# An in projection with tokens stationary, in groups of four tiles, turned by VectorE and a scratch buffer

## The chip, the cores and the metric

The kernel runs on one core of one Trainium2 chip. The metric is device time in microseconds (us) of one execution, as the median of several runs. The engines are TensorE (PE; PEld is its weight load), VectorE (DVE), ScalarE (ACT), GpSimd (POOL) and SyncE (SP), which issues most transfers. SBUF is the working memory, PSUM holds matmul sums.

## The reference, cut to what matters

One decoder layer over 256 tokens with 2,048 features, all in float32: a mixer, a memory cross-attention and a SwiGLU FFN, each behind an RMS norm, with residual adds and a last norm. The change lies in the mixer:

```python
proj = h @ w_in                                  # h: (256, 2048), w_in: (2048, 11296)
z, xbc, dt_raw, sc_u, sc_b, sc_c = split(proj)   # 2048, 3072, 32, 2048, 2048, 2048
xbc = silu(causal_dwconv(xbc, ssd_conv_w) + ssd_conv_b)       # 4 taps along the tokens
xs, bm, cm = split(xbc)                          # 2048, 512, 512
y = ssd_chunked(xs, softplus(dt_raw + dt_bias), -exp(a_log), bm, cm) + xs * d_skip
y_ssd = grouped_rmsnorm(y * silu(z), ssd_norm, 4)
v = sc_b * causal_dwconv(sc_c * sc_u, sc_conv_w)              # 3 taps
y_sc = grouped_rmsnorm(v, sc_norm, 16)
h = h + concatenate([y_ssd, y_sc]) @ w_out       # w_out: (4096, 2048)
```

## The kernel before, in words

**Precision.** Every float32 factor is split into a high part, rounded to the fp32r format, and a low part, the rest. A product is made as high x high + low x high + high x low, in fp32r matmuls summed in PSUM.

**The weight stream.** All weights come in one stream of blocks of 128 x 1024 floats (512 KB), in the order of `stream_plan` (L69). `load_to` (L146) issues the loads on SP, up to `AHEAD` = 6 blocks ahead into 6 raw buffers. `split_to` (L157) makes each block's high part on ACT (L167) and its low part on DVE (L168), with 4 buffers for each.

**Units.** The work is a row of units (`unit`, L273) of two blocks each. A unit issues loads, splits and its matmuls; after its first part it calls `step` (L253), which moves every running process (a Python generator, one for each chain of later work) on to its next `yield`. A `yield` so means "one unit later", and it is counted by hand so that what a chain puts on PE finds its data ready. PE and SP run in program order as written (L114); the order on ACT, DVE and POOL is made by the framework's scheduler.

**The in projection** (L718 to L778) makes 88 tiles of 128 features x 256 tokens, features on partitions. The order is `mixer_order` (L47): for each of 4 head groups its B and C tile, then z and xs tiles, and between them short convolution tiles (c, u, b). The first four tiles, `FIRST`, run in halves of K. For a tile the weights are stationary. For each of 16 blocks of K, `mm_hi` (L293, matmul at L296) multiplies the weights' high part with the tokens' high and low parts at once (512 columns: 256 of each), and `mm_lo` (L298, L302) multiplies the weights' low part with the tokens' high part (256 columns). A tile takes one PSUM buffer of 512 columns, of which there are 4 (`acc`). `evac_sum` (L191) adds its two halves: a copy on ACT (L194) and an addition on DVE (L195).

**The chains behind a tile.** `conv_post` (L610; four taps, L614 to L618), `z_post` (L718), `scc_post`, `scu_post`, `scb_post` (L742 to L771), `b_post`, `c_post` and `xs_post` (L621 to L698). They put small single precision matmuls on PE, between the parts of later units: turns of xs tiles (L660), score products (L634), the scan (L676, L678), and for the norms turns (L202, in `flip`) and broadcasts (L244, in `bcast`). `norm_group` (L700) ends by writing features for the out projection into `ys`: 0 to 15 from the heads, 16 to 31 from the short convolutions. The last short convolutions have fewer yields, so that they end in time.

**The out projection** (L898) takes 4 column blocks n of 512; for each, 16 weight blocks c, block c reading `ys[2c]` and `ys[2c + 1]`. Here tokens are stationary and weights move (`tok_mm`, L791): for each half of a block and each of two token blocks three matmuls of 512 columns (L798 to L800), into two PSUM buffers. `wo_post` adds the residual (L814), and for blocks 0 to 2 turns the result onto features: `turn_blocks` (L818, transposes of 32 x 32 blocks on DVE, L822) into one of 2 buffers, `put` (L825) writes 512 KB to a scratch buffer in DRAM, and `get` (L831) reads it back in four transfers of 128 KB with features on partitions. The gate and up stage (L1074) uses the same `tok_mm` and, behind each up block, the same three steps.

Of the kernel before, what the change touches and what calls it, by code (L numbers as in the profile page):

```python
# [13 lines left out]
F32 = mybir.dt.float32  # L14
# [6 lines left out]
T = 256  # L21
# [21 lines left out]
UT, SBT, SCT = 0, 16, 32  # L43
FIRST = (BT, CT, ZT, ZT + 1)


def mixer_order():  # L47

    o, sc = [], iter(range(16))

    def short_conv():
        j = next(sc)
        return [("scc", "b", SCT + j, j), ("scu", "b", UT + j, j), ("scb", "b", SBT + j, j)]

    for g in range(4):
        if g:
            o += [("B", "a", BT + g, g), ("C", "a", CT + g, g)]
        for t in range(4 * g, 4 * g + 4):
            if ZT + t not in FIRST:
                o.append(("z", "a", ZT + t, t))  # L60
            o.append(("xs", "a", XT + t, t))
            if t % 4:
                o += short_conv()
    for _ in range(4):
        o += short_conv()
    return o


def stream_plan():  # L69

    p = []
    p += [(("k0",), 512), (("v0",), 512)]
    for kt in range(1, KT):
        p.append((("kv", kt), 1024))
    p += [(("a", t, c), 1024) for c in range(2) for t in FIRST]
    for _, m, t, _ in mixer_order():
        p += [((m, t, c), 1024) for c in range(2)]
    for n in range(4):
        p += [(("wo", n, c), 1024) for c in range(KT)]
    p += [(("q", t, c), 1024) for c in range(2) for t in range(4)]  # L80
    p += [(("o", n, c), 1024) for n, c in [(0, 0), (1, 0), (0, 1), (1, 1), (2, 0), (2, 1), (3, 0), (3, 1)]]
    for n in range(FN):
        for m in "gu":
            p += [((m, n, c), 1024) for c in range(KT // 2)]
    for n in range(4):
        p += [(("d", n, c), 1024) for c in range(FT // 2)]
    return p


def trunk(tc, wst, vecs, xp, xtp, mp, wdt_in, nfin, outp):  # L90
# [9 lines left out]
    with ExitStack() as ctx:  # L100
# [139 lines left out]
        def bcast(r):  # L240
# [5 lines left out]
            return ps  # L246


        now = [0]
# [48 lines left out]
        def mm_lo(ps, key, acts, k0, stop):  # L298
            _, l = fin(key)
            n = plan[index[key]][1] // 128  # L300
            for k in range(n):
                mm(ps[:, 0:T], l[:, k * 128:k * 128 + 128], acts[k0 + k][:, 0:T], start=False, stop=stop and k == n - 1)  # L302

        def pair_parts(a, b):

            def los_():
                mm_lo(*a[:4], a[5])
                mm_lo(*b[:4], b[5])

            return [([a[1], b[1]], lambda: mm_hi(*a[:5])), ([b[1]], lambda: mm_hi(*b[:5])), ([a[1], b[1]], los_)]  # L310

# [308 lines left out]

        def b_post(g, ps):  # L621
            bct[g] = slot()
            conv_post(ps, 16 + g, bct[g][:, 0:T], ("B", g))
            return
            yield

        def c_post(g, ps):
            conv_post(ps, 20 + g, bct[g][:, T:], ("C", g))
            yield
# [20 lines left out]

        def xs_post(g, j, ps):
            t = 4 * g + j
            xs = slot()
            conv_post(ps, t, xs[:, 0:T], ("xs", t))
            yield
# [44 lines left out]
        def norm_group(items, sums, sq, n, key):  # L700
            r = inv_rms(sums(sq), n)
            yield
            if key != ("sc", 15):
                yield
            rb = bcast(r)
# [22 lines left out]
        def std_unit(m, t, post):  # L728

            ps = acc()  # L730
            unit(pair_parts((ps, (m, t, 0), xn, 0, True, False), (ps, (m, t, 1), xn, 8, False, True)), post(ps))

        fps = [acc() for _ in FIRST]
        for c in range(2):
            for i in (0, 2):
                posts = [b_post(0, fps[0]), c_post(0, fps[1])] if i == 0 else [z_post(0, fps[2]), z_post(1, fps[3])]
                unit(pair_parts(*[(fps[k], ("a", FIRST[k], c), xn, 8 * c, c == 0, c == 1) for k in (i, i + 1)]),
                     posts if c else None)

        scc, scv = {}, {}  # L740

        def scc_post(j, ps):  # L742
            c = slot()
            evac_sum(ps, c[:, 0:T])
            scc[j] = c
            return
            yield

        def scu_post(j, ps):
            u = tmp()  # L750
            evac_sum(ps, u)
            c = scc[j]
            tt(u, u, c[:, 0:T], ALU.mult)
            a = c[:, T:]
            ts(a, u, v("sw", 3 * j + 2), None, ALU.mult)
# [6 lines left out]

        def scb_post(j, ps):
            u = tmp()
            evac_sum(ps, u)
            a = scv[j]
            tt(a, a, u, ALU.mult)
            yield
            if j < 14:
                yield  # L770
            yield from norm_group([(a, v("nsc", j), 16 + j)], feature_squares, a, 128, ("sc", j))  # L771

        posts = {"B": b_post, "C": c_post, "z": z_post, "scc": scc_post, "scu": scu_post, "scb": scb_post,
                 "xs": lambda t, ps: xs_post(t // 4, t % 4, ps)}
        for kind, m, t, j in mixer_order():
            if kind == "B":
                procs.append(decay(j))
            std_unit(m, t, lambda ps: posts[kind](j, ps))  # L778

# [10 lines left out]

        def tok_mm(ps, key, blocks, tbs, start, stop, ks=(0, 1)):  # L791

            h, l = fin(key)
            for i in ks:
                w = slice(i * 512, i * 512 + 512)
                for tb in tbs:
                    ah, al = blocks(i, tb)
                    mm(ps[tb], ah, h[:, w], start=start and i == ks[0], stop=False)  # L798
                    mm(ps[tb], ah, l[:, w], start=False, stop=False)  # L799
                    mm(ps[tb], al, h[:, w], start=False, stop=stop and i == ks[-1])  # L800

        def side_blocks(tiles, k0):

            def blocks(i, tb):
                a = tiles[k0 + i]
                return a[:, tb * 128:tb * 128 + 128], a[:, T + tb * 128:T + tb * 128 + 128]

            return blocks

        def add_to_res(n, accs, sums):  # L810

            for tb in range(2):
# [3 lines left out]
                act(j, h, AF.Square, accum_out=sums[:, tb, n:n + 1])  # L816

        def turn_blocks(src):  # L818

            t = bp.tile([128, 1024], F32, tag="b", name=nm("b"))  # L820
            for tb in range(2):
                nc.vector.transpose(t[:, tb * 512:tb * 512 + 512], src[tb])  # L822
            return t

        def put(t):  # L825

            w = drp.tile([2, 128, 512], F32, tag="w", name=nm("w"), bufs=2)
            nc.sync.dma_start(w.rearrange("t p k -> p t k"), t.rearrange("p (t k) -> p t k", t=2))
            return w

        def get(w):  # L831


            d = fp.tile([128, 1024], F32, tag="f", name=nm("f"))
            for b in range(4):
                nc.sync.dma_start(d[32 * b:32 * b + 32, :].rearrange("p (x c) -> p x c", x=8),
                                  w.rearrange("t (a i) k -> i (t a) k", a=4)[:, :, 128 * b:128 * b + 128])
            return d.rearrange("p (x f j) -> p f x j", x=8, f=4)

# [57 lines left out]

        for n in range(4):  # L898
            accs = [acc(), acc()]
            for c in range(0, KT, 2):  # L900
                unit([([("wo", n, k)],
                       lambda k=k: tok_mm(accs, ("wo", n, k), side_blocks(ys, 2 * k), (0, 1), k == 0, k == KT - 1))
                      for k in (c, c + 1)], wo_post(n, accs) if c == KT - 2 else None)

# [310 lines left out]
def _weights(i):  # L1215
# [8 lines left out]
    blk["a"] = tiles(w_in[:, 0:5120], 8)  # L1224
    blk["b"] = tiles(w_in[:, 5152:], 8)
    blk["q"] = tiles(_turned(np.asarray(i["w_q"])[0], 3), 8)
    rows = {m: (_turned(np.asarray(i[k])[0]) if m == "d" else np.asarray(i[k])[0]).reshape(-1, 2, 128, i[k].shape[-1] // 512, 512).transpose(3, 0, 2, 1, 4)
            for m, k in (("wo", "w_out"), ("o", "w_o"), ("g", "w_gate"), ("u", "w_up"), ("d", "w_down"))}
    wk, wv = np.asarray(i["w_k"])[0], np.asarray(i["w_v"])[0]
    plan = stream_plan()  # L1230
    out = np.empty(sum(128 * w for _, w in plan), np.float32)
    p = 0
    for key, w in plan:
        m = key[0]
        if m == "k0":
            c = wk[0:128]
# [58 lines left out]
```

## Time and profile before

| what | value |
|---|---|
| median of 3 runs | 1544.58 us (1544.18 to 1544.87) |
| the profiled execution: its own time | 1543.5 us |
| the profiled execution: its span | 1541.8 us |
| in projection, from the span's start | about 54.5 to 581.7 us |
| out projection | about 581.7 to 757 us |

The span is what the trace covers; the execution's own time has 1.7 us more around it. The page gives each engine's busy time, the granted clock of PE, the chain of work that ended last and groups of instructions; other views give the waits, the instructions in order of time and busy times by window. A duration of a PE matmul is modelled and overlaps the next one's, so PE's pace is read from the distance between starts. Lines such as L296 are lines of the kernel before.

### The profile page before, as it was taken

The numbers are of one execution on the slowest core, as the hardware profiler recorded it, in microseconds if no ns is written. First come the engines' busy times: TensorE is split into PE (matmuls) and PEld (weight loads), VectorE is DVE, ScalarE is ACT, GpSimd is POOL, SyncE is SP. The second block draws the span as 40 slices with busy tenths as digits, with TensorE's granted clock in tenths as the row PEclk, the third lists the DMA queues.
The fourth block names the chain that finished last, engine by engine and source line by source line (L and its number), as shares of the span: only waits on it lengthen the run. The fifth ranks groups of instructions, "written<-read, shape, count | busy, mean of one in ns | idle before, by whom it ended". The sixth has DMA issues, their size and how long they took to land.

```text
span 1541.8 us, 20228 instructions
## 1 busy us (share of the span) xinstructions
PE 1528.6 (99%) x7607; PEld 1282.6 (83%) x7607; DVE 930.3 (60%) x1239; ACT 807.0 (52%) x1158; POOL 44.9 (3%) x65
## 2 busy tenths in 40 slices
PE   9999999999999999999999999999999999999997
PEld 7888888888888888888888888888888888888886
DVE  5967786786776675555566555555455555455453
ACT  6685774775774454444465444444444444444343
POOL 0001300100100000000000000000000000000000
PEclk9999999999999999999999999999999999999999
DMA  9765655655655556777645666666766666656652
GB/s 349 251 201 186 218 176 180 217 178 177 209 186 168 181 173 208 237 235 231 193 134 180 218 219 224 214 206 202 232 221 221 218 227 198 239 192 195 196 193 96
DMA packets 112001, 315.33 MB, mean 205 GB/s; under 512 B 11008, under 2 KB 33952, under 8 KB 111904
## 3 DMA queue, kind: packets, MB, share of 16 engines
q1 hardware_dynamic: 102704, 306.66, 61.1%
q10 hardware_dynamic: 9200, 7.39, 1.6%
q8 instruction: 59, 0.97, 0.3%
q14 instruction: 38, 0.31, 0.1%
HBM read 304.53 MB, written 9.49 MB: 204 GB/s over the span
## 4 chain that ended last, share of the span: by engine, by line
PE 95%; DMA 1%; ACT 1%; issue 1%; SPq 0%; DVE 0%; POOLq 0%; POOL 0%; ACTq 0%
PE a L296 22%; PE a L800 20%; PE a L799 20%; PE a L798 20%; PE a L302 11%; DMA r<-in_w_dram 1%; PE m L676 1%; ACT h L167 0%; PE m L202 0%; PE m L244 0%; PE a L518 0%; PE m L868 0%; PE m L678 0%; PE m L660 0%; PE m L926 0%
## 5 line engine op out<-in xcount | busy, mean ns | idle before, releaser
L168 DVE TENSOR_TENSOR l<-r,h 128x1024 fp32r<-128x1024 f32 (+2 forms) x555 | 656.0, 1191 | 509.1 <-ACT h L167 419.9
L167 ACT CAST h<-r 128x1024 fp32r<-128x1024 f32 (+2 forms) x555 | 564.7, 1022 | 617.2 <-PE a L800 463.3
L798 PE MATMUL a<-h,s 128*128 128x512 f32 x1343 | 524.1, 390 | 0.0
L800 PE MATMUL a<-h,s 128*128 128x512 f32 x1343 | 522.7, 389 | 0.0
L799 PE MATMUL a<-l,s 128*128 128x512 f32 x1343 | 522.6, 389 | 0.0
L296 PE MATMUL a<-s,h 128*128 128x512 f32 x1472 | 370.4, 397 | 0.3 <-ACT h L167 0.3
L296 PEld LDWEIGHTS a<-s,h 128*128 128x128 f32 x1472 | 265.5, 188 | 52.9 <-issue 2.6
L800 PEld LDWEIGHTS a<-h,s 128*128 128x128 f32 x1343 | 252.1, 188 | 52.3
L799 PEld LDWEIGHTS a<-l,s 128*128 128x128 f32 x1343 | 252.1, 188 | 52.1
L798 PEld LDWEIGHTS a<-h,s 128*128 128x128 f32 x1343 | 252.1, 188 | 52.0
L302 PEld LDWEIGHTS a<-s,l 128*128 128x128 f32 x1472 | 188.9, 191 | 7.8
L302 PE MATMUL a<-s,l 128*128 128x256 f32 x1472 | 191.4, 282 | 0.0
L194 ACT COPY t<-a 128x256 f32<-128x256 f32 x96 | 35.1, 369 | 37.0 <-PE a L302 36.7
L617 DVE SCALAR_TENSOR_TENSOR t<-t,vec,t 128x255 f32<-128x255 f32 (+2 forms) x72 | 34.7, 482 | 6.1 <-ACT t L614 5.3
L237 POOL TENSOR_TENSOR rr<-rv,half 128x2 f32<-128x2 f32 x24 | 16.6, 692 | 643.5 <-DVE rv L236 626.6
L195 DVE TENSOR_TENSOR t<-a,t 128x256 f32<-128x256 f32 x76 | 31.8, 418 | 5.2 <-ACT t L194 4.0
L518 PE MATMUL a<-s,h 128*128 128x512 f32 x64 | 23.9, 404 | 1.0 <-DVE s L182 0.5
L1123 POOL TENSOR_TENSOR fr<-fr,half 128x1 f32<-128x1 f32 x2 | 1.1, 550 | 716.8 <-DVE fr L1122 716.8
L1049 ACT ACTIVATE g<-a,fscale 128x512 f32<-128x512 f32 x22 | 15.0, 689 | 9.9 <-PE a L800 9.9
L519 PE MATMUL a<-s,l 128*128 128x256 f32 x64 | 18.4, 287 | 0.7 <-DVE l L168 0.7
L236 DVE TENSOR_SCALAR rv<-rv 128x2 f32<-128x2 f32 x24 | 4.0, 168 | 24.4 <-ACT t L229 24.1
L618 ACT ACT_TABLE_LOAD x12 | 15.4, 1283 | 6.2 <-DVE t L617 3.1
(172 smaller groups left out, 683.2 us busy)
## 6 DMA issues: line engine op xcount, KB each, us to landing
r<-in_w_dram SPq DMA_DIRECT2D x535, 512.0 KB, 4.1
w<-b SPq DMA_DIRECT2D x14, 512.0 KB, 3.3
f<-w SPq DMA_DIRECT2D x56, 128.0 KB, 4.4
s<-acsT ACTq DMA_DIRECT2D x24, 256.0 KB, 6.3
s<-in_xt_dram SPq DMA_DIRECT2D x16, 256.0 KB, 6.0
s<-in_x_dram SPq DMA_DIRECT2D x8, 256.0 KB, 7.2
s<-in_m_dram SPq DMA_DIRECT2D x7, 256.0 KB, 7.2
s<-in_nfin_dram SPq DMA_DIRECT2D x4, 256.0 KB, 7.5
```

What stands on the lines that cost most here:

```text
L167: nc.scalar.copy(h[:, c], r[:, c])
L168: tt(l[:, c], r[:, c], h[:, c].bitcast(F32), ALU.subtract)
L194: nc.scalar.copy(t, ps[:, T:])
L195: tt(dst, ps[:, 0:T], t, ALU.add)
L296: mm(ps, h[:, k * 128:k * 128 + 128], acts[k0 + k], start=start and k == 0, stop=False)
L302: mm(ps[:, 0:T], l[:, k * 128:k * 128 + 128], acts[k0 + k][:, 0:T], start=False, stop=stop and k == n - 1)
L518: mm(kacc[t], h[:, t * 128:t * 128 + 128], a, start=s, stop=False)
L519: mm(kacc[t][:, 0:T], l[:, t * 128:t * 128 + 128], a[:, 0:T], start=False, stop=e)
L617: stt(a[:, d:], u[:, 0:T - d], v("cw", 4 * ct + k), a[:, d:], ALU.mult, ALU.add)
L798: mm(ps[tb], ah, h[:, w], start=start and i == ks[0], stop=False)
L799: mm(ps[tb], ah, l[:, w], start=False, stop=False)
L800: mm(ps[tb], al, h[:, w], start=False, stop=stop and i == ks[-1])
```

## The change

- `mixer_groups` replaces `mixer_order`: the same 88 tiles in the same order, the four of `FIRST` at the head, cut into 22 groups of four.
- The weights of a group are laid out as 512 columns, permuted on the host so that DVE's 32 x 32 transposes and the strided read give whole features. A group has 8 blocks, each with two blocks of K.
- Each group runs through `tok_mm` into two PSUM buffers, in 4 units. Groups 0 and 1 alternate by halves of K.
- Behind a group, `group_post` turns the sums (one unit later), writes them (one later), reads them back (one later) and starts the four tiles' chains, one per unit, or all four at once for the last three groups.
- `evac_sum` goes from the in projection's chains. `conv_post` copies its tile from the read-back buffer on ACT; z, c, u and b read it in place. The shortened yields of the last short convolutions go.
- `turn_blocks` has 1 buffer in place of 2, `get` 3 in place of 2.
- The out projection reads blocks c = 0 to 13 of n = 0 and of n = 1, then c = 14 and 15 of both, then n = 2 and 3 as before.

```diff
-def mixer_order():
+def mixer_groups():
...
-    return o
+    return [o[i:i + 4] for i in range(0, len(o), 4)]
+
+def out_order():
+    return ([(n, c) for n in range(2) for c in range(14)] + [(n, c) for n in range(2) for c in (14, 15)]
+            + [(n, c) for n in (2, 3) for c in range(KT)])
...
-        bp = E(tc.tile_pool(name="blocks", bufs=2))
-        fp = E(tc.tile_pool(name="feat", bufs=2))
+        bp = E(tc.tile_pool(name="blocks", bufs=1))
+        fp = E(tc.tile_pool(name="feat", bufs=3))
...
-        def conv_post(ps, ct, dst, key):
+        def conv_post(src, ct, dst, key):
             u = tmp()
-            evac_sum(ps, u)
+            nc.scalar.copy(runs(u), src)
...
-        def z_post(t, ps):
-            u = tmp()
-            evac_sum(ps, u)
+        def z_post(t, src):
             sz = slot()[:, 0:T]
-            act(sz, u, AF.Silu)
+            act(runs(sz), src, AF.Silu)
...
-            tt(u, u, c[:, 0:T], ALU.mult)
+            tt(runs(u), src, scc.pop(j), ALU.mult)
...
+        def group_post(n, accs):
+            t = turn_blocks(accs)
+            yield
+            w = put(t)
+            yield
+            d = get(w)
+            yield
+            for f, (kind, _, _, j) in enumerate(groups[n]):
+                p = posts[kind](j, d[:, f])
+                if next(p, 0) is None:
+                    procs.append(p)
+                if f < 3 and n < paces:
+                    yield
+
+        def in_units(n, accs, cs):
+            for c in cs:
+                unit([([("in", n, k)], lambda k=k: tok_mm(accs, ("in", n, k), side_blocks(xn, 2 * k), (0, 1),
+                                                        k == 0, k == KT // 2 - 1)) for k in (c, c + 1)],
+                     group_post(n, accs) if c == KT // 2 - 2 else None)
+
+        first = [[acc(), acc()] for _ in range(2)]
+        for cs in ((0, 2), (4, 6)):
+            for n in range(2):
+                in_units(n, first[n], cs)
+        for n in range(2, len(groups)):
...
+            in_units(n, [acc(), acc()], range(0, KT // 2, 2))
...
+        waccs = {}
+        for n, c in out_order()[::2]:
+            if c == 0:
+                waccs[n] = [acc(), acc()]
+            unit([([("wo", n, k)], lambda k=k: tok_mm(waccs[n], ("wo", n, k), side_blocks(ys, 2 * k), (0, 1),
+                                                    k == 0, k == KT - 1)) for k in (c, c + 1)],
+                 wo_post(n, waccs[n]) if c == KT - 2 else None)
```

More of the change, by code (lines that the diff above doesn't have):

```diff
@@ L43 @@
 UT, SBT, SCT = 0, 16, 32
-FIRST = (BT, CT, ZT, ZT + 1)
-def mixer_order():
-    o, sc = [], iter(range(16))
+def mixer_groups():
+    o = [("B", "a", BT, 0), ("C", "a", CT, 0), ("z", "a", ZT, 0), ("z", "a", ZT + 1, 1)]
+    sc = iter(range(16))
     def short_conv():
@@ L58, in mixer_order @@
         for t in range(4 * g, 4 * g + 4):
-            if ZT + t not in FIRST:
+            if t > 1:
                 o.append(("z", "a", ZT + t, t))
@@ L74, in stream_plan @@
         p.append((("kv", kt), 1024))
[L75 to L79, printed above, removed]
+    p += [(("in", n, c), 1024) for h in range(2) for n in range(2) for c in range(4 * h, 4 * h + 4)]
+    for n in range(2, 22):
+        p += [(("in", n, c), 1024) for c in range(KT // 2)]
+    p += [(("wo", n, c), 1024) for n, c in out_order()]
     p += [(("q", t, c), 1024) for c in range(2) for t in range(4)]
@@ L246, in bcast, with tok_mm, side_blocks, blocks @@
             return ps
+        def tok_mm(ps, key, blocks, tbs, start, stop, ks=(0, 1)):
+            h, l = fin(key)
+            for i in ks:
+                w = slice(i * 512, i * 512 + 512)
+                for tb in tbs:
+                    ah, al = blocks(i, tb)
+                    mm(ps[tb], ah, h[:, w], start=start and i == ks[0], stop=False)
+                    mm(ps[tb], ah, l[:, w], start=False, stop=False)
+                    mm(ps[tb], al, h[:, w], start=False, stop=stop and i == ks[-1])
+        def side_blocks(tiles, k0):
+            def blocks(i, tb):
+                a = tiles[k0 + i]
+                return a[:, tb * 128:tb * 128 + 128], a[:, T + tb * 128:T + tb * 128 + 128]
+            return blocks
+        def turn_blocks(src):
+            t = bp.tile([128, 1024], F32, tag="b", name=nm("b"))
+            for tb in range(2):
+                nc.vector.transpose(t[:, tb * 512:tb * 512 + 512], src[tb])
+            return t
+        def put(t):
+            w = drp.tile([2, 128, 512], F32, tag="w", name=nm("w"), bufs=2)
+            nc.sync.dma_start(w.rearrange("t p k -> p t k"), t.rearrange("p (t k) -> p t k", t=2))
+            return w
+        def get(w):
+            d = fp.tile([128, 1024], F32, tag="f", name=nm("f"))
+            for b in range(4):
+                nc.sync.dma_start(d[32 * b:32 * b + 32, :].rearrange("p (x c) -> p x c", x=8),
+                                  w.rearrange("t (a i) k -> i (t a) k", a=4)[:, :, 128 * b:128 * b + 128])
+            return d.rearrange("p (x f j) -> p f x j", x=8, f=4)
         now = [0]
@@ L608, in trunk, with runs @@
         bct = {}
-        def conv_post(ps, ct, dst, key):
+        def runs(a):
+            return a.rearrange("p (x j) -> p x j", x=8)
+        def conv_post(src, ct, dst, key):
             u = tmp()
-            evac_sum(ps, u)
+            nc.scalar.copy(runs(u), src)
             a = tmp()
@@ L702, in norm_group @@
             yield
-            if key != ("sc", 15):
-                yield
+            yield
             rb = bcast(r)
@@ L726, in z_post, with scc_post, scu_post @@
             yield
[L728 to L738, printed above, removed]
         scc, scv = {}, {}
[L742 to L745, printed above, removed]
+        def scc_post(j, src):
+            scc[j] = src
             return
             yield
-        def scu_post(j, ps):
+        def scu_post(j, src):
             u = tmp()
-            evac_sum(ps, u)
-            c = scc[j]
-            tt(u, u, c[:, 0:T], ALU.mult)
-            a = c[:, T:]
+            tt(runs(u), src, scc.pop(j), ALU.mult)
+            a = slot()[:, 0:T]
             ts(a, u, v("sw", 3 * j + 2), None, ALU.mult)
@@ L761, in scu_post, with scb_post @@
             yield
-        def scb_post(j, ps):
-            u = tmp()
-            evac_sum(ps, u)
+        def scb_post(j, src):
             a = scv[j]
-            tt(a, a, u, ALU.mult)
+            tt(runs(a), runs(a), src, ALU.mult)
             yield
-            if j < 14:
-                yield
+            yield
             yield from norm_group([(a, v("nsc", j), 16 + j)], feature_squares, a, 128, ("sc", j))
         posts = {"B": b_post, "C": c_post, "z": z_post, "scc": scc_post, "scu": scu_post, "scb": scb_post,
[L774 to L778, printed above, removed]
+                 "xs": lambda t, src: xs_post(t // 4, t % 4, src)}
+        groups = mixer_groups()
+        paces = len(groups) - 3
+        def group_post(n, accs):
[4 more added lines that the diff above has]
+            d = get(w)
+            yield
+            for f, (kind, _, _, j) in enumerate(groups[n]):
[3 more added lines that the diff above has]
+                if f < 3 and n < paces:
+                    yield
+        def in_units(n, accs, cs):
[8 more added lines that the diff above has]
+        for n in range(2, len(groups)):
+            for kind, _, _, j in groups[n]:
+                if kind == "B":
+                    procs.append(decay(j))
+            in_units(n, [acc(), acc()], range(0, KT // 2, 2))
         res = [[None] * 4 for _ in range(2)]
@@ L789, in trunk @@
                 ahead_of(index[("wo", n, 8 + 2 * tb)], lambda tb=tb, n=n: load_res(tb, n))
[L791 to L808, printed above, removed]
         def add_to_res(n, accs, sums):
@@ L816, in add_to_res @@
                 act(j, h, AF.Square, accum_out=sums[:, tb, n:n + 1])
[L818 to L838, printed above, removed]
         def gained(src, gain, t):
@@ L1228, in _weights @@
             for m, k in (("wo", "w_out"), ("o", "w_o"), ("g", "w_gate"), ("u", "w_up"), ("d", "w_down"))}
+    groups = []
+    for g in mixer_groups():
+        c = np.concatenate([w_in[:, (0 if m == "a" else 5152) + 128 * t:][:, 0:128] for _, m, t, _ in g], axis=1)
+        c = _turned(c.T).T
+        groups.append(c.reshape(8, 2, 128, 512).transpose(0, 2, 1, 3))
     wk, wv = np.asarray(i["w_k"])[0], np.asarray(i["w_v"])[0]
@@ L1234, in _weights @@
         m = key[0]
-        if m == "k0":
+        if m == "in":
+            c = groups[key[1]][key[2]]
+        elif m == "k0":
             c = wk[0:128]
```

25 lines of the change are left out of this document (6 added, 19 removed).

## The prediction

> **What bounds the kernel now.** I read the page first: the engines, the clock row, the chain that ended last.
>
> ```profile
> span 1541.8 us, 20228 instructions
> PE 1528.6 (99%) x7607; PEld 1282.6 (83%) x7607; DVE 930.3 (60%) x1239; ACT 807.0 (52%) x1158; POOL 44.9 (3%) x65
> PEclk9999999999999999999999999999999999999999
> PE 95%; DMA 1%; ACT 1%; issue 1%; SPq 0%; DVE 0%; POOLq 0%; POOL 0%; ACTq 0%
> ```
>
> TensorE (PE) carries 95% of the chain at the full granted clock. PE's matmul ends are modelled, so "busy" does not say that its pace is the best one. Hence the second view, windows by stage: the in projection, the out projection, most of gate and up.
>
> ```profile
> core 0: us, PE busy (x) PEld busy (x) DVE busy (x) ACT busy (x) POOL busy (x), PEclk, DMA share, GB/s
> 54.50:581.70 527.20, 526.87 (x3117) 453.89 (x3117) 382.81 (x628) 339.24 (x559) 39.91 (x51) 1.00 0.59 190
> 581.70:757.00 175.30, 175.30 (x778) 145.10 (x778) 93.91 (x101) 78.29 (x100) 0.69 (x1) 1.00 0.71 221
> 830.00:1290.00 460.00, 460.00 (x2031) 380.90 (x2030) 243.53 (x230) 203.61 (x212) 0.00 (x0) 1.00 0.67 217
> ```
>
> In the in projection VectorE (DVE) is busy for 73% (382.81 of 527.20) and ScalarE (ACT) for 64%. Third, the waits inside that stage: PE's own, and the longest one of ACT.
>
> ```profile
> PE a L296 <- ACT h L167: 0.3, 1, 0.3
> ACT h L167 <- PE a L296: 111.5, 81, 2.7
> ```
>
> PE waited 0.3 us in 527; the engine that splits weights waited for PE, 81 times. So this stage lasts as long as PE's list of instructions, and a change to it is worth what it does to that list, unless it creates a wait.
>
> **The list before.** The chain in order of time shows two undisturbed output tiles (start, duration, what).
>
> ```profile
> 62.46 3.65 PE a L296 x16
> 66.11 1.91 PE a L302 x16
> 68.02 3.65 PE a L296 x16
> 71.68 1.91 PE a L302 x16
> 73.59 1.85 PE a L296 x8
> ```
>
> From 62.46 to 73.59 are 11.13 us for two tiles, 5.565 each: 16 matmuls of 512 columns at 228 ns (3.65/16) and 16 of 256 columns at 119.4 ns (1.91/16). Two of the short ones take 239 ns for the columns of one long one. A group of four tiles costs 4 x 5.565 = 22.26 us, and 88 tiles make 489.7 us. The rest of the 527.2, 37.5 us, is single precision work between the tiles (turns, broadcasts, the scan) with its switches.
>
> **The list after.** Four tiles become one group of 512 features: 8 weight blocks, each with 2 halves x 2 token blocks x 3 products, so 96 matmuls of 512 columns instead of 64 of 512 and 64 of 256. The sum of columns is the same (49,152); there are 32 instructions fewer. Stationary tokens and moving weights are the form of gate and up, whose window shows 460.00/2031 = 226.5 ns for a matmul, with two starts of its timeline confirming it:
>
> ```profile
> 900.05 0.39 PE L798 MATMUL a<-h,s 128*128 128x512 f32 x1
> 900.73 0.39 PE L798 MATMUL a<-h,s 128*128 128x512 f32 x1
> ```
>
> Three in 0.68 us are 226.7 ns. 96 x 226.6 ns = 21.75 us for a group. The gain is 22.26 - 21.75 = 0.51 us a group, over 22 groups **11.2 us**. A page's rule gives far less: the Trainium skill ("TensorE: Matmul & The Clock Gate", Back-to-back issue gap) puts the spacing at N/2.4 + 2.5 ns, by which 32 saved matmuls are 0.08 us a group and 1.8 us in all. The rows disagree with it here: 119.4 ns stands where it has 109, 226.6 where it has 216.
>
> The work between the tiles stays: a switch into single precision and back costs the same in both forms. Before and in the out projection:
>
> ```profile
> 164.35 2.00 PE L296 MATMUL a<-s,h 128*128 128x512 f32 x8
> 168.24 2.08 PE L302 MATMUL a<-s,l 128*128 128x256 f32 x16
> 595.65 0.39 PE L800 MATMUL a<-h,s 128*128 128x512 f32 x1
> 596.33 0.40 PE L799 MATMUL a<-l,s 128*128 128x512 f32 x1
> ```
>
> The first pair holds 16 long matmuls and a broadcast: 3.89 - 3.65 = 0.24 us. The second holds two long ones and a broadcast: 0.68 - 0.45 = 0.23 us. The code has 76 of them (16 turns and 16 scan steps of head tiles, 4 score products, 20 sums and 20 broadcasts); 0.01 to 0.03 us of difference each, either way, bounds this at -2 to +2 us. I take 0.
>
> **What leaves ACT and DVE.** Each tile loses its evacuation, a copy on ACT and an addition on DVE.
>
> ```profile
> L194 ACT COPY t<-a 128x256 f32<-128x256 f32 x88 | 32.4, 369 | 36.2 <-PE a L302 35.9
> L195 DVE TENSOR_TENSOR t<-a,t 128x256 f32<-128x256 f32 x71 | 29.7, 419 | 5.2 <-ACT t L194 4.0
> L822 DVE STREAM_TRANSPOSE b<-g x22: 665/685/703, 859.6 to 1295.4; 128x512 f32<-128x512 f32 x22
> L814 DVE TENSOR_TENSOR s<-a,s x16: 676/682/692, 625.7 to 814.2; 128x512 f32<-128x512 f32 x16
> L846 ACT ACTIVATE s<-f,vec x12: 496/496/507, 643.5 to 731.8; 128x256 fp32r<-128x256 f32 x12
> ```
>
> DVE loses 88 x 0.419 = 36.9 us and gains 44 transposes. Those of before read SBUF (685 ns); the new ones read PSUM, which no row shows. L814, as wide and reading PSUM, has 682, so I take 685, 30.1 us, with bounds from 0.67 to 0.75. ACT loses 32.5 us and gets 24 copies for the four-tap convolution, now from a strided SBUF tile; between the 369 of L194 and the 496 of L846 I take 430, 10.3 us. So DVE goes from 382.8 to about 376 in a stage of 516 us, and ACT to 317. Neither is nearer to being the bound on average.
>
> **What is added to SP and DMA.** For each group one 512 KB write and four 128 KB reads, in SP's ordered queue together with the weight loads. The gate and up stage has the same sequence, once in 16 weight blocks; now it comes once in 8.
>
> ```profile
> 852.95 3.05 SPq L153 DMA_DIRECT2D r<-in_w_dram  x2
> 860.92 0.38 SPq L828 DMA_DIRECT2D w<-b  x1
> 861.39 1.30 SPq L153 DMA_DIRECT2D r<-in_w_dram  x2
> 864.11 1.81 SPq L836 DMA_DIRECT2D f<-w  x4
> SPq L828 <- DVE b L822: 49.1, 10, 4.9
> SPq L836 <- DMA w<-b: 14.8, 10, 1.6
> DMA to landing us min/median/max: 3.5/4.4/8.5
> r<-in_w_dram SPq DMA_DIRECT2D x535, 512.0 KB, 4.1
> GB/s 349 251 201 186 218 176 180 217 178 177 209 186 168 181 173 208 237 235 231 193 134 180 218 219 224 214 206 202 232 221 221 218 227 198 239 192 195 196 193 96
> ```
>
> Behind the waiting write stand weight loads: up to 4.9 us there, 1.6 at the read, 1.8 to issue it, about 8 us in the worst group. Loads run 6 blocks ahead, 6 x 2.72 = 16.3 us, and land in 4.1; 12 us of cover hide 8. In gate and up PE waited for none of it (460.00 busy of 460.00). Traffic: 4.19 MB of weights and 0.52 + 0.52 MB of scratch (the write and the reads) in 21.75 us are 241 GB/s, against 190 in the stage before and 349 in the page's first slice (its GB/s row). Nothing is charged. If this cover were gone, PE would wait for a block, at most its 4.1 us landing, in some groups.
>
> **The added waits.** The transposes wait for a group's last matmul. Behind them on DVE are the low parts (L168) of the next weight blocks, for which PE waits two blocks later. Gate and up shows that place, with two products of 0.7 us ahead of the transposes as well:
>
> ```profile
> 857.14 1.22 DVE L168 TENSOR_TENSOR l<-r,h 128x1024 fp32r<-128x1024 f32 x1 [1.49 <-ACT h L167]
> 858.28 1.40 DVE L1057 SCALAR_TENSOR_TENSOR g<-a,fscale,g 128x512 f32<-128x512 f32 x2
> 859.60 1.29 DVE L822 STREAM_TRANSPOSE b<-g 128x512 f32<-128x512 f32 x2
> 860.82 1.18 DVE L168 TENSOR_TENSOR l<-r,h 128x1024 fp32r<-128x1024 f32 x1
> 862.58 1.22 DVE L168 TENSOR_TENSOR l<-r,h 128x1024 fp32r<-128x1024 f32 x1 [0.58 <-ACT h L167]
> ```
>
> 2.5 us there put one low part late by under a microsecond, and the second is already back in step. Here 1.3 us of transposes meet one convolution or gate chain of the group before (one per unit by the pacing), where before 0.42 us of addition met the same chain. I charge 0; a stall of 0.1 us in each group, 2 us, is in the range.
>
> The chains of a group now start four units (22 us) after its last matmul. At the end of the stage this could expose the out projection. Counting units from its first (0), the last head group's features are made in units 2 and 3 and read in unit 3; group 21's tiles are turned in unit 0, written in 1, read in 2, used in 3, and the last short convolution's features are made in unit 8. They belong to block 15, which the new order reads in unit 14: 6 units of slack, where the old order would read them in unit 7. Unit 3 is the tight one: DVE makes features 14 and 15 about 3 us before PE needs them, by the lead it has over PE. Block 2's accumulators are freed by two additions (0.68 each) in unit 15 and needed in unit 16, 5.4 us later. I charge 0, with 3 us for one slip. The out projection's 768 matmuls only change order.
>
> **The sum.** 11.2 us off the profiled execution's 1543.5 us (1541.8 of span and 1.7 around it) gives 1532.3. The median of the runs, 1544.58, stands 1.08 above that execution, so **1533.4 us**. About 0.2% (3 us) is what a measurement here tells from no change.
>
> **Rivals.** (a) *The round trip comes late in some groups.* With twice the scratch transfers per block, the reads land nearer the 8.5 us maximum than the 4.4 median; ACT and DVE, in order, wait for them. At 0.25 us of PE wait in each group half the gain goes: 1539 us. For it: these queues were never loaded this densely for 500 us. Against: the 12 us of cover above.
> (b) *DVE's burst reaches PE: slower.* The transposes (1.37 us) take the place of one addition (0.42) right behind the last matmul. If DVE has no slack left there, the low parts and so PE are 0.95 us late in each group: 22 x (0.95 - 0.51) = +9.7, 1554.3 us. It decides from 0.51 us per group on, and is measurably slower from 0.65. For it: DVE's 73% is an average, with bursts for the scan. Against: the quoted burst of 2.5 us that PE did not feel, and ACT's 111.5 us of waiting for PE, which is the lead.
> (c) *Columns alone set the pace.* If a matmul in this stage costs what its columns cost in the old form, the 49,152 columns keep their 22.26 us, 231.9 ns for each of the 96, and nothing changes: 1544.6 us. For it: the stage has more DVE and ACT traffic than gate and up, and its long matmuls ran at 228. Against: even at 228 they give 21.9, a gain of 8 us. The Trainium skill's spacing rule above would come out near this one too, at 1542.8.
> (d) *Smaller waits eat the whole gain*: 0.5 us a group from (a) and (b) together, 1544.6 us.
>
> **Chances.** Forecast (1530 to 1537) 0.78; (a) 0.08; (b) 0.07; (c) 0.03; (d) 0.04. Faster by over 0.2% is the forecast and (a), 0.86; within 0.2% is (c) and (d), 0.07; slower is (b), 0.07. The range reaches from 1530.5 (merged interruptions, the pace of 226.5) to 1540 (case a), which holds 0.86.
>
> **What would show it.** The in projection's matmuls at L-lines of the token form, spaced 226 to 228 ns, 2,112 of them; 96 in about 21.8 us where nothing lies between; the stage near 516 us instead of 527.2; 44 transposes of about 0.69 us; PE's waits still below 1 us in that stage; out projection still near 175 us. I am wrong if PE waits for L167 or L168 once in each group (b), for features in the out projection's first units, or if the spacing comes out above 230 ns (c).

## The result, and the profile after

| | before | after |
|---|---|---|
| median (us) | 1544.38 (4 runs, 1543.61 to 1544.87) | 1533.45 (4 runs, 1532.43 to 1533.91) |
| ratio after/before | | 0.9929, 95% interval 0.9912 to 0.9946 |
| span of the profiled execution | 1541.8 | 1531.8 |

The changed kernel is faster by 10.9 us (0.7%). Its lines have moved: `tok_mm` is now L260 to L262, the high and low parts of a weight block are made at L172 and L173, `turn_blocks` is L276, `put` L282, `get` L290. First its page: span, engines, clock and chain.

```profile
span 1531.8 us, 18911 instructions
PE 1518.1 (99%) x6903; PEld 1246.6 (81%) x6903; DVE 928.7 (61%) x1195; ACT 757.9 (49%) x1070; POOL 52.5 (3%) x65
PEclk9999999999999999999999999999999999999999
PE 96%; DMA 2%; issue 1%; ACT 1%; DVE 0%; SPq 0%; POOLq 0%; POOL 0%; ACTq 0%
```

PE has 704 matmuls fewer (22 groups x 32) and is still the whole chain. Next, the stages of the changed kernel by window: in projection, out projection, both together; behind them both together for the kernel before. The bounds are the first matmul of the in projection, of the out projection and of the query projection.

```profile
core 0: us, PE busy (x) PEld busy (x) DVE busy (x) ACT busy (x) POOL busy (x), PEclk, DMA share, GB/s
57.40:570.75 513.35, 513.35 (x2376) 416.17 (x2373) 373.58 (x561) 285.60 (x456) 45.46 (x49) 1.00 0.76 237
570.75:746.50 175.75, 175.75 (x783) 145.53 (x782) 99.56 (x118) 81.43 (x112) 2.78 (x4) 1.00 0.73 230
57.41:746.51 689.10, 689.10 (x3158) 561.70 (x3155) 473.14 (x677) 367.03 (x568) 48.24 (x52) 1.00 0.75 235
```

```profile
56.37:756.59 700.22, 699.89 (x3862) 597.70 (x3859) 474.44 (x721) 416.16 (x656) 40.60 (x52) 1.00 0.62 198
```

The two stages went from 700.22 to 689.10 us, 11.12 less, and in both of them PE no longer waits for anything: its busy time is the window. What lies behind them takes 785.2 us before and 785.3 after. What lies ahead (56.37 and 57.41) differs by 1.04 us in these two executions, though the programs are the same there; over the kernels below the stage began anywhere between 56.37 and 58.28, with no relation to the edit (58.28, 56.87 and 58.11 in three kernels that differ only behind it). It is a stretch in which the transfers are busy all the time, and weight loads are the largest part of the chain that ended last (38.6% of its first 60 us):

```profile
20.00:40.00 20.00, 19.41 (x98) 15.83 (x97) 13.79 (x25) 16.80 (x36) 0.70 (x1) 1.00 1.04 398
```

The length of the two stages is therefore the finer measure, and it is given for each experiment as "the two stages". It comes from one execution; the program after it (the same in all kernels) took 785.2 to 785.4 in each, so the two stages carry each kernel's difference apart from the start.

The in projection's pace, in a stretch without other work on PE:

```profile
412.15 0.39 PE L260 MATMUL a<-h,s 128*128 128x512 f32 x1
412.83 0.39 PE L260 MATMUL a<-h,s 128*128 128x512 f32 x1
413.51 0.39 PE L260 MATMUL a<-h,s 128*128 128x512 f32 x1
414.19 0.39 PE L260 MATMUL a<-h,s 128*128 128x512 f32 x1
```

Three in 0.68 us, 226.7 ns each, in each of the three steps: the pace of gate and up. On the other engines (groups of the changed kernel, then, in the second fence, two of the table loads before):

```profile
L276 DVE STREAM_TRANSPOSE b<-a x44: 667/708/717, 93.3 to 571.3; 128x512 f32<-128x512 f32 x44
L276 DVE STREAM_TRANSPOSE b<-s x6: 669/702/711, 654.9 to 705.6; 128x512 f32<-128x512 f32 x6
L653 ACT COPY t<-f 128x256 f32<-128x256 f32 x24 | 9.5, 396 | 0.0
L659 ACT ACT_TABLE_LOAD x4 | 5.1, 1283 | 0.4 <-DVE t L658 0.4
L640 ACT ACT_TABLE_LOAD x3 | 3.8, 1283 | 0.1
```

```profile
L618 ACT ACT_TABLE_LOAD x12 | 15.4, 1283 | 6.2 <-DVE t L617 3.1
L602 ACT ACT_TABLE_LOAD x12 | 15.4, 1283 | 0.2
```

The transposes that read PSUM take 708 ns in the median. Those that read SBUF take 685 in gate and up, but 702 in the out projection, so the source does not decide. DVE has 373.6 us of work in the stage. ACT has 285.6, far less than before (339.2): the evacuations went, and 13 loads of function tables stand where 37 stood. Last, SP's queue around one group:

```profile
314.19 0.38 SPq L282 DMA_DIRECT2D w<-b  x1
314.67 1.41 SPq L158 DMA_DIRECT2D r<-in_w_dram  x2
317.84 1.80 SPq L290 DMA_DIRECT2D f<-w  x4
319.75 13.00 SPq L158 DMA_DIRECT2D r<-in_w_dram  x6
```

Between the pair of loads and the next six lie 3.7 us, and the write before them had waited too; the loads catch up within the group. The longest stretch of the stage in which no weight load is issued is 6.4 us (192.2 to 198.6).

### The profile page after: what moved, and what is told of

Its sections match the earlier page's. It is cut to its first block, busy times and chain, and to the rows that moved or that the text cites. A ratio compares the mean times of both kernels' runs of the same rounds, so it can differ in the third digit from the quotient of the medians.

```text
span 1531.8 us, 18911 instructions
## 1 busy us (share of the span) xinstructions
PE 1518.1 (99%) x6903; PEld 1246.6 (81%) x6903; DVE 928.7 (61%) x1195; ACT 757.9 (49%) x1070; POOL 52.5 (3%) x65
## 4 chain that ended last, share of the span: by engine, by line
PE 96%; DMA 2%; issue 1%; ACT 1%; DVE 0%; SPq 0%; POOLq 0%; POOL 0%; ACTq 0%
PE a L260 30%; PE a L262 30%; PE a L261 30%; DMA r<-in_w_dram 2%; PE a L342 1%; PE m L717 1%; PE a L348 0%; PE m L207 0%; PE m L249 0%; PE a L556 0%; PE m L876 0%; ACT h L172 0%; PE m L701 0%; PE m L719 0%; PE m L935 0%
## 5 line engine op out<-in xcount | busy, mean ns | idle before, releaser
L173 DVE TENSOR_TENSOR l<-r,h 128x1024 fp32r<-128x1024 f32 (+2 forms) x555 | 658.8, 1190 | 534.4 <-ACT h L172 510.0
L172 ACT CAST h<-r 128x1024 fp32r<-128x1024 f32 (+2 forms) x555 | 566.0, 1023 | 693.6 <-PE a L262 619.1
L260 PE MATMUL a<-h,s 128*128 128x512 f32 x2047 | 805.2, 393 | 0.0
L262 PE MATMUL a<-h,s 128*128 128x512 f32 x2047 | 797.8, 390 | 0.0
L261 PE MATMUL a<-l,s 128*128 128x512 f32 x2047 | 797.7, 390 | 0.0
L262 PEld LDWEIGHTS a<-h,s 128*128 128x128 f32 x2047 | 384.3, 188 | 80.9
L260 PEld LDWEIGHTS a<-h,s 128*128 128x128 f32 x2047 | 384.4, 188 | 80.6 <-issue 2.4
L261 PEld LDWEIGHTS a<-l,s 128*128 128x128 f32 x2047 | 384.6, 188 | 77.7
L276 DVE STREAM_TRANSPOSE b<-a 128x512 f32<-128x512 f32 x44 | 29.7, 700 | 2.0 <-PE a L262 1.9
L556 PE MATMUL a<-s,h 128*128 128x512 f32 x64 | 23.9, 404 | 1.4 <-DVE s L187 1.1
L557 PE MATMUL a<-s,l 128*128 128x256 f32 x64 | 18.4, 287 | 0.8 <-DVE l L173 0.8
L556 PEld LDWEIGHTS a<-s,h 128*128 128x128 f32 x64 | 12.0, 188 | 5.8 <-DVE s L187 2.3
L342 PE MATMUL a<-s,h 128*128 128x512 f32 x64 | 16.5, 400 | 0.0
L781 DVE SCALAR_TENSOR_TENSOR s<-t,vec,s 128x255 f32<-128x255 f32 (+1 forms) x32 | 16.1, 506 | 0.4
L640 ACT ACTIVATE s<-s,nacs 128x256 f32<-128x256 f32 x32 | 16.0, 499 | 0.0
```

Of the source, the lines that this page charges most:

```text
L172: nc.scalar.copy(h[:, c], r[:, c])
L173: tt(l[:, c], r[:, c], h[:, c].bitcast(F32), ALU.subtract)
L342: mm(ps, h[:, k * 128:k * 128 + 128], acts[k0 + k], start=start and k == 0, stop=False)
L556: mm(kacc[t], h[:, t * 128:t * 128 + 128], a, start=s, stop=False)
L557: mm(kacc[t][:, 0:T], l[:, t * 128:t * 128 + 128], a[:, 0:T], start=False, stop=e)
L781: stt(a[:, d:], u[:, 0:T - d], v("sw", 3 * j + k), a[:, d:], ALU.mult, ALU.add)
```

## The experiments

The theory: each matmul carries a fixed cost beside its columns, and the gain is 704 of these costs, with a slightly better pace of the long matmuls. Rivals: columns alone count and the gain is from elsewhere (the order of the out projection, the spacing of the chains, the relief of ACT); and, for the margins, that DVE's burst or the scratch round trip is nearly felt.

**One product cut in two.** It restores the matmul count and widths of the kernel before, with tokens still stationary. In the in projection's copy of `tok_mm`:

```diff
-                    mm(ps[tb], al, h[:, w], start=False, stop=stop and i == ks[-1])
+                    for c in (0, 256):
+                        mm(ps[tb][:, c:c + 256], al, h[:, i * 512 + c:i * 512 + c + 256], start=False, ...)
```

> The changed kernel, with one of the three products of each token block and half (low tokens x high weights) cut into two matmuls of 256 columns in the in projection. A group then has 64 matmuls of 512 and 64 of 256 columns, the count and widths of the kernel before, but still with tokens stationary. Theory (each matmul carries a fixed cost of about 12.2 ns beside its columns: 2 x 119.4 - 226.6): 704 more matmuls, +8.6 us, 1542 us. Rival one (columns alone set the pace, the gain came from somewhere else): unchanged, 1533.5. Rival two (a fixed cost of 2.5 ns): +1.8 us, 1535.2.

1543.13 us, 0.9992 of the kernel before (0.9983 to 1.0002): the gain is all but gone. The two stages took 698.61 us, 9.51 more than in the changed kernel, for 704 matmuls: 13.5 ns each.

```profile
56.93:755.54 698.61, 698.61 (x3862) 597.97 (x3859) 471.75 (x677) 364.88 (x566) 50.85 (x52) 1.00 0.74 232
```

ACT is as relieved (364.88) as in the changed kernel and the scratch round trip is there: neither is where the gain came from. Of the 11.12 us 1.6 stayed (698.61 against 700.22).

**Two products cut in two.** The same edit on the second product (`ah`, `l`) as well.

> As the run with one product cut in two, but with two of the three products cut (high tokens x low weights as well): 1,408 more matmuls than the changed kernel, 160 in a group. Theory (fixed cost of 12.2 ns): +17.2 us, 1550.6 us, slower than the kernel before. Columns alone: 1533.5. A fixed cost of 2.5 ns: 1537.

1551.72 us, 1.0048 of before (1.0033 to 1.0063); the two stages 707.55 us, 18.45 more for 1,408 matmuls, 13.1 ns each. Twice the matmuls, twice the loss, and no columns were added: columns alone are ruled out. Each added matmul brings a weight load of its own (with one product cut 3,859 in the two stages, in the changed kernel 3,155), so the 13 ns are the price of the two together; no run takes them apart. The Trainium skill's fixed 2.5 ns ("TensorE: Matmul & The Clock Gate", Back-to-back issue gap), which that section gives for a matmul without its weight load, does not hold for these fp32r matmuls with theirs.

**The out projection's order alone**, in the kernel before.

```diff
-    for n in range(4):
-        p += [(("wo", n, c), 1024) for c in range(KT)]
+    p += [(("wo", n, c), 1024) for n, c in out_order()]
```

> The kernel before with one part of the change alone: the out projection reads blocks 14 and 15 of its first two column blocks last. Theory (the order only makes room for later chains, PE does not wait before either): 1544.4 us, within 0.1%. Rival (the new order itself takes a wait or interruption off the out projection): lower by 2 us or more.

1544.32 us, ratio 1.0001 (0.9991 to 1.0011); the two stages 700.23 against 700.22. The order brings nothing and costs nothing; it makes room.

**The round trip twice.**

```diff
             w = put(t)
+            w2 = drp.tile([2, 128, 512], F32, tag="w2", name=nm("w"), bufs=2)
+            nc.sync.dma_start(w2.rearrange("t p k -> p t k"), t.rearrange("p (t k) -> p t k", t=2))
             yield
             d = get(w)
+            for e in range(2):
+                d2 = gtp.tile([128, 512], F32, tag="g", name=nm("g"))
+                for b in range(4):
+                    nc.sync.dma_start(d2[32 * b:32 * b + 32, :]..., w2...[:, 4 * e:4 * e + 4, 128 * b:128 * b + 128])
```

> The changed kernel with the scratch round trip of each group of the in projection made twice: a second write of 512 KB to another scratch buffer and a second read of it, in eight transfers of 64 KB, into buffers nobody reads. Traffic of the stage rises from 236 to about 285 GB/s. Theory (12 us of cover in the weight stream hide the queue's waits): 1533.5 us, within 1.5 us. Rival a (the round trip is nearly late already): PE waits in each group, at 0.25 us a group +5.5 us, 1539, with waits of PE for L172 or L173 in the trace.

1587.41 us, 1.0283 of before (1.0267 to 1.0299): the theory was wrong by 54 us, and the rival by 48. SP's queue around one group, PE's waits in the stage, and one window:

```profile
299.29 1.58 SPq L158 DMA_DIRECT2D r<-in_w_dram  x2
306.35 1.80 SPq L290 DMA_DIRECT2D f<-w  x4
308.20 6.13 SPq L810 DMA_DIRECT2D g<-w  x8
314.43 2.81 SPq L158 DMA_DIRECT2D r<-in_w_dram  x6
PE a L260 <- ACT h L172: 15.8, 8, 3.4
PE a L261 <- DVE l L173: 15.3, 17, 2.8
200.00:300.00 100.00, 87.54 (x361) 68.21 (x360) 59.67 (x92) 40.20 (x63) 6.50 (x9) 0.90 0.69 208
```

From 300.9 to 314.4 no weight load is issued: the reads wait for their writes and then need 1.8 and 6.1 us to issue. That is 13.6 us, more than the 12 us of cover. But PE does not wait behind it: its wait before ends at 297.22, and the next one ends at 348.19. This hold was not felt. What PE waits for are high and low parts that ACT and DVE make late, and in all but one of the 25 waits not because weights landed late: the one that follows a late landing is of 0.3 us, at 432.6, behind 4.1 us that ACT waited for a block. The first fence has three waits of these engines in the changed kernel, the second the same three here, both from 57 to 600 us:

```profile
ACT h L172 <- DMA r<-in_w_dram: 9.6, 6, 1.9
ACT s L659 <- DVE t L658: 1.0, 3, 0.4
DVE b L276 <- PE a L262: 1.9, 3, 1.3
```

```profile
ACT h L172 <- DMA r<-in_w_dram: 10.0, 6, 4.1
ACT s L659 <- DVE t L658: 55.3, 17, 6.6
DVE b L276 <- PE a L262: 29.4, 16, 5.2
```

In sum ACT waits for weight loads as long as in the changed kernel. What is new is that ACT waits for DVE's convolutions, and DVE, at the transposes, for PE. The order of the work on ACT and DVE, which the framework's scheduler makes, is another one here. In the changed kernel DVE makes seven low parts (L173) between 222.6 and 242.6 us, 2.7 to 3.7 us apart, with the chains' work between them. Here the transposes and ten instructions of the chains stand between one low part and the next, and PE waits:

```profile
222.78 1.23 DVE L173 TENSOR_TENSOR l<-r,h 128x1024 fp32r<-128x1024 f32 x1 [1.49 <-ACT h L172]
226.72 1.40 DVE L276 STREAM_TRANSPOSE b<-a 128x512 f32<-128x512 f32 x2 [2.72 <-PE a L262]
236.60 2.36 DVE L173 TENSOR_TENSOR l<-r,h 128x1024 fp32r<-128x1024 f32 x2 [1.78 <-ACT h L172]
236.62 0.79 PE L260 MATMUL a<-h,s 128*128 128x512 f32 x1 [2.74 <-ACT h L172]
238.89 0.63 PE L260 MATMUL a<-h,s 128*128 128x512 f32 x1
240.17 0.63 PE L260 MATMUL a<-h,s 128*128 128x512 f32 x1
```

The last two rows show a second price, the clock: three matmuls take 1.28 us there, 427 ns each in place of 226.7, and the granted clock of the 100 us window is 0.90. The Trainium skill ("TensorE: Matmul & The Clock Gate", Part 1) says that an idle stretch of some microseconds takes the array back to half its clock. The 427 ns agree with the half.

So this run does not price the second trip by itself. The order on ACT and DVE changed with it, no run kept the order, and where the cover of the weight stream ends is not shown.

**The same bytes without the waits.** The second write as above; the second read from a buffer written once, in two transfers.

```diff
+            if n > 1:
+                for e in range(2):
+                    d2 = gtp.tile([128, 512], F32, tag="g", name=nm("g"))
+                    nc.sync.dma_start(d2, w3[0][e])
```

> The changed kernel with about the bytes of the doubled round trip, but without its waits: a second write of 512 KB as there, and a second read of 512 KB in two transfers of 256 KB from a scratch buffer that was written once at the start, into buffers nobody reads. Theory (in the doubled trip the weight loads stood 13.6 us behind the ordered queue's waits and issues, more than their 12 us of cover): here the queue is held for about 2 us more per group, so 1533.5 us, within 2 us, at some 285 GB/s. Rival (the traffic itself starves the weight stream): PE waits as with the doubled trip, 1550 us or more.

1539.6 us, 0.9969 of before (0.9958 to 0.998); the two stages 695.80 us, 6.70 more than in the changed kernel, at 264 GB/s.

```profile
56.59:752.39 695.80, 692.47 (x3159) 562.18 (x3156) 471.02 (x677) 363.88 (x568) 48.60 (x52) 1.00 0.82 264
```

Both sides missed: the theory allowed 2 us and the kernel took 6.1 more, the rival wanted 16. PE waits four times in the two stages, 3.3 us in all. The order on ACT and DVE is another one here too (ACT waits 38.3 us for DVE at L659, from 57 to 600 us, against 1.0 in the changed kernel). So the 6.7 us cannot be put down to the bytes, nor the 48 us between the two kernels to the waits and small reads of the doubled trip.

**Transposes three times, and five times.**

```diff
             t = turn_blocks(accs)
+            for _ in range(2):                       # 4 in the second run
+                for tb in range(2):
+                    nc.vector.transpose(t[:, tb * 512:tb * 512 + 512], accs[tb])
```

> The changed kernel with the two transposes behind each group made three times over (four more, 2.7 us of DVE, right behind the group's last matmul). Theory (DVE runs ahead of PE by more than its burst, and the stage is PE's list): unchanged, within 2 us of 1533.5. Rival b (DVE's burst is felt on PE): the added 2.7 us appear in each group, up to +60 us, 1593; if the slack is about 1 us, +37 us.

> The changed kernel with the two transposes behind each group made five times over (eight more, 5.5 us of DVE behind each group's last matmul, DVE at about 97% of the stage). Theory: the lead of up to four blocks is used up, PE waits in some groups, between +5 and +40 us; the point at which the burst is felt lies between this and the run with three. Rival b: already felt with three, and here +120 us.

1535.71 us (0.9947 of before, 0.993 to 0.9963) and 1559.14 us (1.0099, 1.0084 to 1.0114). With three turns the median is 2.2 us above 1533.5, just outside the 2 that were allowed, and the two stages took 691.12 us, 2.02 more; five turns lie inside their range, with DVE busy for 86% of the stage and not 97. The only wait of PE with three, and PE's waits with five:

```profile
PE a L261 <- DVE l L173: 1.5, 1, 1.5
```

```profile
PE a L261 <- DVE l L173: 17.8, 11, 3.9
```

2.7 us of extra DVE work behind each group were felt once in 22 groups, 5.5 us in half of them. So the margin differs by group: it is over 2.7 us in 21 of them and over 5.5 in 11. Rival (b) of the prediction, which had it at nothing, is ruled out. (The added transposes take 676 ns in the median, from the same PSUM.)

**All four chains of a group in one unit.** `paces = 0`.

> The changed kernel with all four chains of a group started in the same unit, in place of one per unit. Theory (bursts on ACT and DVE below the lead of the splits are not felt): within 3 us of 1533.5; some PE waits for L172 or L173 of about a microsecond may show. Rival (the even spacing of the chains is what keeps the burst behind a group off PE): a wait of 1 us or more in most groups, +20 us or more.

1530.47 us, 0.9915 of before (0.99 to 0.993). The two stages took 686.61 us, 2.49 less than in the changed kernel. Neither side expected a gain. PE shows where it is: single precision work of two chains falls together. The changed kernel, one scan step with a turn behind it and then one alone:

```profile
155.61 0.39 PE L262 MATMUL a<-h,s 128*128 128x512 f32 x1
157.25 0.39 PE L261 MATMUL a<-l,s 128*128 128x512 f32 x1
162.26 0.39 PE L262 MATMUL a<-h,s 128*128 128x512 f32 x1
163.72 0.40 PE L261 MATMUL a<-l,s 128*128 128x512 f32 x1
```

and the unpaced one, two scan steps and a turn:

```profile
155.04 0.39 PE L262 MATMUL a<-h,s 128*128 128x512 f32 x1
157.32 0.39 PE L261 MATMUL a<-l,s 128*128 128x512 f32 x1
```

Alone a scan step takes 163.72 - 162.26 - 2 x 0.227 = 1.01 us; behind another it adds 2.28 - 1.64 = 0.64. Three pairs of scan steps came together so, and eleven turns stand behind a scan step in place of two (a turn there adds 1.64 - 1.46 = 0.18, alone 0.26). By these prices that makes 3 x 0.37 + 9 x 0.08 = 1.8 of the 2.49 us; the rest was not traced.

**Groups 0 and 1 one after the other.** The alternation of halves is taken out of the loop and the stream.

> The changed kernel without alternating the halves of groups 0 and 1: all 8 blocks of group 0, then all of group 1. Theory (the normed tokens are made by DVE well ahead, since PE waited 0.3 us in the stage before with the same demand): unchanged, within 1 us of 1533.5. Rival (the second half of the tokens is not ready 11 us into the stage): one wait of 2 to 8 us at the stage's start.

1532.61 us, 0.9929 of before (0.9914 to 0.9944); the two stages 689.11 against 689.10. The alternation does nothing.

**Both edits, and then more or fewer interruptions.** The last two change only the yields of a short convolution's norm.

```diff
             r = inv_rms(sums(sq), n)
-            yield
-            yield
+            for _ in range(4 if key[0] == "sc" else 2):     # 1 in the other, with two yields more ahead of the sum
+                yield
```

> The changed kernel with both edits that came out faster or equal: all four chains of a group started in one unit, and groups 0 and 1 not alternated. Single precision work interrupts PE's long matmuls 70 times here, counted in the program over all stages, 84 times in the changed kernel. Theory (each interruption costs PE about 0.15 us beside its own matmuls): 1530.5 us. Rival (starting the chains together helps in another way, and not alternating adds 0.9 us): 1529.6.

> As the unpaced and not alternated kernel, with two more units between the sum and the broadcast of a short convolution's norm, so that more of this work falls together: 61 interruptions in place of 70, the same matmuls. Theory (0.15 us each): 1529.1 us, faster than both kernels. Rival (the number of interruptions is not what matters): 1530.5.

> As the unpaced and not alternated kernel, with two more units ahead of a short convolution's sum and one less ahead of its broadcast, so that this work falls apart: 82 interruptions in place of 70, the same matmuls. Theory (0.15 us each): 1532.3 us, though the chains still start together. Rival (starting the chains together is what helped): 1530.5.

With 70 interruptions 1531.69 us (0.9918 of before, 0.9905 to 0.9932), with 61 1529.99 us (0.9907, 0.9894 to 0.9921), with 82 1534.05 us (0.994, 0.9928 to 0.9953). The medians fit 0.2 us an interruption, but the stages do not: 686.65, 686.34 and 690.83 us. From 70 to 61 only 0.3 us went, since turns and broadcasts that merge with one another save almost nothing (a broadcast alone 0.24, two together 0.47). And the third has something else in it:

```profile
297.08 0.50 PE L259 MATMUL a<-h,s 128*128 128x512 f32 x1 [1.54 <-ACT h L171]
298.34 0.50 PE L260 MATMUL a<-l,s 128*128 128x512 f32 x1 [0.76 <-DVE l L172]
```

a stall of PE for the parts of a weight block, some 2.8 us with its restart. So the theory of one price per interruption fell: what counts is which work falls together. The kernel with 61 has the lowest median, 0.5 us below the unpaced one and 3.5 below the changed one; they were not all run on the same chip, and their intervals overlap.

## Why the prediction was right

- **PE's list is the bound.** Right. PE waits 0.3 us in the stage before and for nothing in the two stages after.
- **The pace, 11.2 us.** The two stages lost 11.12 us, the medians 10.9. The two cuts show the cause: the matmuls put back cost 13.1 to 13.5 ns each, where the prediction's rows gave 12.2. At 13.3, 704 of them make 9.4 of the 11.1 us. With the count restored 1.6 us of the gain stayed. That is near what the 228 ns of the old long matmuls against 226.6 would give (1,408 x 1.4 ns = 2.0), but that part was not tested alone. Rival (c), columns alone, is out.
- **The work between the tiles stays.** Right in sum. The in projection itself lost more, from 525.4 us (56.37 to 581.77) to 513.35, and the out projection gained 0.9 (175.75 against 174.82): four turns and broadcasts of the last chains moved across, at 0.24 us each.
- **ACT and DVE.** DVE is busy for 373.6 us (predicted 376). The new transposes take 708 ns (685), the copies 396 (430). ACT was missed, 285.6 against 317: the prediction did not think of the 24 table loads of 1.283 us that went, 30.8 us. Nothing hung on it.
- **The queue.** The charge of nothing was right: with up to 6.4 us between weight loads PE waits for nothing in the changed kernel, so rival (a) did not come about, nor (d). Where the 12 us of cover end stays open: even a hold of 13.6 us in the doubled trip was not felt, and that kernel's 54 us came with another order on ACT and DVE.
- **The added waits.** Right: the three-fold transposes show a margin of over 2.7 us in all groups but one, so (b) is out. PE waited for no feature in the out projection's first units either.
- **The predicted median**, 1533.4 against 1533.45, is closer than the method can be, and so in part luck: the stretch ahead of the in projection alone moves by 1.9 us between executions.

## What to carry to other kernels

Where one engine is busy without a wait, count its instructions and not only its columns: price both forms by the distance between starts, from rows of the same kernel, and the difference is the gain. Where a scheduler orders the work of some engines, a test that adds transfers or instructions can change that order too: compare what these engines wait for in both kernels before the added work is given the blame, as the doubled round trip showed. Small single precision work between long matmuls is cheaper when its matmuls stand together, but only some kinds: look at the pair before counting it.

## What the runs showed of the hardware

- A fixed cost of 13.1 to 13.5 ns for each fp32r matmul with its weight load, beside its columns, nearly the same for 704 and 1,408 added ones.
- A scan step of eight small matmuls costs PE 1.01 us alone and 0.64 us behind another; merged broadcasts save about 0.01 us.
- Waits of PE of up to 3.4 us each, in a 100 us window with 12.5 us of idle time, went with a mean granted clock of 0.90; behind one of them matmuls of 512 columns started 427 ns apart in place of 226.7.
- A 128x512 transpose on DVE takes 676 to 708 ns in the median from PSUM and 685 to 702 from SBUF.
